# Hybrid decoder layer on one core: two weight passes of a feature chunk merged, a new chunk order, and units emitted by a clock per engine

## The chip, the cores and the metric

The kernel runs on one core of one Trainium2 chip. The core's engines each have an instruction queue of their own that is worked off in order: PE (matrix multiply), DVE (vector), ACT (activations), POOL (general purpose) and SP (which here only issues DMAs). The metric is the device time of one execution in microseconds (us), the median of several runs.

## The reference

One decoder layer over 256 tokens of width 1024, in float32. The tokens are RMS-normalised and multiplied by one wide input projection, whose columns feed three gated branches and three merge gates; each branch is projected back to 1024, the branches are summed under sigmoid gates, and an output projection, a residual add and a last RMSNorm follow.

```python
h = rms_norm(x, norm_g[layer])
(qa, ka, va, ga, ub, vb, gb, qc, gc, ma, mb, mc) = split_cols(h @ w_in[layer], IN_SPLITS)
qa = partial_rope(qa.reshape(B, S, MOBA_HEADS, HEAD_DIM), pos)
ka = partial_rope(ka.reshape(B, S, MOBA_HEADS, HEAD_DIM), pos)
va = va.reshape(B, S, MOBA_HEADS, HEAD_DIM)
out_a = moba_attention(qa, ka, va) * jax.nn.silu(ga)
out_b = gmlp_spatial_gate(ub, vb, gmlp_ln_g[layer], w_spatial[layer], b_spatial[layer]) * jax.nn.silu(gb)
mem_n = rms_norm(mem, mem_norm_g[layer])
out_c = memory_cross_attention(qc, mem_n, w_mem_kv[layer]) * jax.nn.silu(gc)
y = (jax.nn.sigmoid(ma) * (out_a @ w_branch_a[layer])
     + jax.nn.sigmoid(mb) * (out_b @ w_branch_b[layer])
     + jax.nn.sigmoid(mc) * (out_c @ w_branch_c[layer]))
x = x + y @ w_out[layer]
...
return rms_norm(x, final_norm_g)
```

Branch A has 6 heads of 128 with causal softmax attention (with 256 tokens there is a single block, so it is plain causal attention), branch B mixes 6 groups of 128 channels over chunks of 128 tokens, branch C has 4 heads of cross-attention into 256 memory tokens.

## The kernel before

**Products in three passes.** Every large product is made in a reduced float32 format (float32r). To keep precision, each operand is split into hi (rounded to that format) and lo (the rest), and a product is three passes accumulated in PSUM: hi·hi, hi·lo and lo·hi. The helper `mm3` (line 279) issues the three, so lines 280, 281 and 282 carry nearly all matmuls.

**Chunks.** The weights come from HBM as 52 pieces of two chunks each; a chunk is 128 × 1024 values and is the step of the main loop (line 784). There are 106 chunks. Per chunk, ACT writes hi (line 130), DVE writes lo (line 134), and PE multiplies. The splits run three chunks ahead of PE (`LEAD`), in four buffers of hi and of lo (`SPL`), so the hi of chunk c + 3 can start when PE has left chunk c − 1. The first four chunks are split before the loop.

There are four kinds of chunk. A *token* chunk (`mm_tok`, line 294) holds weights for 512 output columns and a quarter of the depth: the tokens are the stationary operand, the weights stream, 12 passes of 512 columns. A *feature* chunk (`mm_fea`, line 350) holds weights for 128 output features and the whole depth of 1024 in 8 steps of k: the weights are stationary and the 256 tokens stream, so 8 × 3 = 24 passes of 256 columns; the result lies with features on the partitions and is copied out of a PSUM bank by one ACT instruction. *Branch* and *output* chunks (`mm_br`, `mm_out`) stream weights like token chunks. Large products use four PSUM banks (`acc`) in turn, small ones four others (`aux`).

The order of the chunks (lines 251 to 272) is: 12 token chunks for the values of A and B (vvb); then per head q and k of A and two light ones out of ub and ga; then qc, mk (feature), mv (token), gc, gb (feature), 24 token chunks for the merge gates (sig), 16 branch chunks, 8 output chunks. Of these 42 are feature chunks.

The tokens for the first 12 chunks are not yet divided by their row norm (hh, hl); from chunk 12 on, normalised ones (nh, nl) are used. To make them, ACT squares and sums the rows (line 209), the reciprocal root becomes a diagonal, PE broadcasts it (line 226), ACT copies it out (line 228), POOL multiplies (line 421), ACT and DVE make hi and lo (lines 231 and 234).

**Units.** All small work (norms, rotation, attention, gates) is cut into named units. A planner written in Python (`Units`, line 46) decides, while the program is built, where each unit goes into the engines' queues. Before and after the matmuls of each chunk its `slot` goes through the list: a unit is emitted if the units it follows are done by at least `gap` chunks and if its cost, summed per engine, fits the room of one chunk. A unit holds work of several engines at once: the scores of a head, for instance, are matmuls, the maximum on DVE and the exponential on ACT. The rooms and the gaps are:

```python
U = Units(2, (1.3, 1.4, 1.35, 2.5), (0.3, 0.8, 0.6, 1.0))
```

Since each queue is in order, an emitted unit that is not ready holds up all that stands behind it on its engine.

**Activations.** SiLU of the gates ga, gc and gb and the sigmoid of sig are applied by ACT as it copies the product out of PSUM (lines 382, 385 and 322); the softmax uses Exp (line 484) and is normalised on DVE (line 495). ACT loads a table when it changes between such functions.

Of the kernel before, what the change touches and what calls it, by code (L numbers as in the profile page):

```python
# [32 lines left out]
D = 1024  # L33
S = 256
# [10 lines left out]

class Units:
# [5 lines left out]
    def __init__(self, gap, room, slack):  # L52
        self.gap, self.room, self.slack = gap, room, slack
        self.used = [0.0] * 4
        self.todo, self.done = [], {}

    def add(self, name, fn, after=(), cost=(0, 0, 0, 0), gap=None, before=(), first=False):
        unit = (name, fn, tuple(after), cost, self.gap if gap is None else gap, tuple(before))
        self.todo.insert(0 if first else len(self.todo), unit)

    def slot(self, i, pe):

        if not pe:
            self.used = [max(0.0, x - r) for x, r in zip(self.used, self.room)]
        rest = []
        todo, self.todo = self.todo, []
        for u in todo:
            name, fn, after, cost, gap, before = u
            if pe == (cost[0] > 0) and all(a in self.done and self.done[a] + gap <= i for a in after) \
# [5 lines left out]
                self.used = [x + c for x, c in zip(self.used, cost)]  # L75
            else:
                rest.append(u)
        self.todo += rest
# [3 lines left out]
def tile_hybrid_layer(ctx: ExitStack, tc: tile.TileContext, xw, memT, mem, x, fin_g, ln_g, w, w_sp, b_sp, rope, out):  # L82
# [112 lines left out]
    hh = act.tile([128, KD, S], F32R, name="hh", tag="hh")  # L195
    hl = act.tile([128, KD, S], F32R, name="hl", tag="hl")

    def sq_tile():
        return work.tile([128, S], F32, name="sq", tag="sq", bufs=2)
# [11 lines left out]
    def rms_rows(acc, dst):  # L211
        rt = work.tile([128, 2], F32, name="rt", tag="rt")
        nc.scalar.activation(rt, acc, AF.Sqrt, bias=eps, scale=1.0 / D)
        nc.vector.reciprocal(dst, rt)

    def rms_diag(r, name):
        dg = work.tile([128, 2, 128], F32, name="dg", tag="sq", bufs=2)
        for t in range(2):
            nc.vector.tensor_scalar(dg[:, t, :], ident, r[:, t:t + 1], None, op0=OP.mult)
        bc["d" + name] = dg  # L220

    def rms_bcast(name):

        p = bank()
        for t in range(2):
            nc.tensor.matmul(p[:, tsl(t)], ones, bc["d" + name][:, t, :], start=True, stop=True)  # L226
        bc[name] = work.tile([128, S], F32, name="bc", tag="ssq", bufs=2)
        nc.scalar.activation(bc[name], p[:, 0:S], AF.Copy)  # L228
# [23 lines left out]
    for g in range(3):  # L252
        chunks += [("tok", "vvb", g * 512, 2 * i) for i in range(4)]

    light = [("fea", "ub", g) for g in range(GB)] + [("fea", "ga", g) for g in range(HA)]
    for h in range(HA):
        chunks += [("fea", "q", h), ("fea", "k", h)] + light[2 * h:2 * h + 2]
    chunks += [("fea", "qc", h) for h in range(HC)]
    chunks += [("fea", "mk", h) for h in range(HC)]
    chunks += [("tok", "mv", 0, 2 * i) for i in range(4)]  # L260
    chunks += [("fea", "gc", g) for g in range(HC)]
    chunks += [("fea", "gb", g) for g in range(GB)]
# [521 lines left out]
    for c in range(n_br + 4):  # L784
# [3 lines left out]
        if s > 3:  # L788
            split(s)
# [116 lines left out]
```

## Time and profile before

| | |
|---|---|
| median of 3 runs | 331.46 us (331.08 to 537.75) |
| the profiled execution's own time | 330.89 us |
| its span, first to last instruction | 329.1 us |
| mean granted clock of PE | 0.997 |
| busy: PE, DVE, ACT, POOL | 321.7, 222.9, 191.2, 39.7 us |
| read from HBM | 61.55 MB, 190 GB/s over the span |

The profile is of one execution. Busy time is the union of an engine's instructions; matmuls are pipelined, so that a row's mean (285 ns for 256 columns) is longer than the distance to the next one. In a row of a group stand the line, engine, operation, what is written and read, the shape and the count; then busy us in total, mean ns of one, and the engine's idle time just before with what ended it. A row of a line's instructions has the durations in ns as min/median/max, then the first and the last start in us. In a timeline row stand the start and the duration in us.

### The profile page before, as it was taken

The page shows a single profiled execution, that of the slowest core. Times are in us where ns is not written, and L with a number is a line of the kernel's source. Part 1 is how long each engine was busy: PE and PEld are TensorE (multiplying, and loading weights), DVE is VectorE, ACT ScalarE, POOL GpSimd, SP SyncE. Part 2 cuts the span into 40 slices and gives each one's busy share as a digit, 9 for nine tenths or more (in the row PEclk, how much of TensorE's full clock was granted, in tenths as well). Part 3 has the DMA queues.
Part 4 walks back from the last instruction along what each step waited for, and adds up shares of the span by engine and source line. Part 5 has one row for each costly group of instructions (what it writes and reads, how often), then busy time and mean ns, then how long its engine had stood idle before and what let it go on. Part 6 is the DMA issues. An engine that isn't in the chain of part 4 may idle for free.

```text
span 329.1 us, 5062 instructions
## 1 busy us (share of the span) xinstructions
PE 321.7 (98%) x1999; PEld 289.3 (88%) x1999; DVE 222.9 (68%) x339; ACT 191.2 (58%) x315; POOL 39.7 (12%) x42
## 2 busy tenths in 40 slices
PE   8999999999999999999999999999999999999992
PEld 4888899999999999988999988888888888888882
DVE  4965869978867898678694755354435469768552
ACT  4779769465885666546964466535554633533433
POOL 0008210000001090100026430000000000000022
PEclk9999999999999999999999999999999999999998
DMA  7999875564433372533656264655465555463003
GB/s 286 392 423 333 341 295 178 207 209 170 134 127 130 127 257 71 201 136 132 245 177 224 66 223 138 247 159 223 147 238 177 205 187 197 135 247 129 0 1 128
DMA packets 10727, 62.91 MB, mean 191 GB/s; under 512 B 1200, under 2 KB 1584, under 8 KB 4176
## 3 DMA queue, kind: packets, MB, share of 16 engines
q1 hardware_dynamic: 10416, 62.08, 52.1%
q10 hardware_dynamic: 288, 0.52, 0.4%
q8 instruction: 15, 0.25, 0.3%
q14 instruction: 8, 0.07, 0.1%
HBM read 61.55 MB, written 1.05 MB: 190 GB/s over the span
## 4 chain that ended last, share of the span: by engine, by line
PE 97%; DVE 1%; ACT 0%; issue 0%; DVEq 0%
PE acc L280 26%; PE acc L282 26%; PE acc L281 26%; PE acc L309 4%; PE aux L280 3%; PE aux L282 3%; PE aux L281 3%; PE aux L472 2%; PE aux L193 1%; PE aux L641 1%; PE aux L512 0%; PE aux L545 0%; ACT jk L757 0%; PE aux L226 0%; DVE xk L755 0%; DVE xk L777 0%
## 5 line engine op out<-in xcount | busy, mean ns | idle before, releaser
L134 DVE TENSOR_TENSOR lo<-raw,hi 128x1024 fp32r<-128x1024 f32 x102 | 127.6, 1254 | 71.2 <-ACT hi L130 67.4
L130 ACT ACTIVATE hi<-raw 128x1024 fp32r<-128x1024 f32 x102 | 107.6, 1057 | 55.3 <-PE acc L282 47.4
L280 PE MATMUL acc<-nh,hi 128*128 128x256 f32 x304 | 86.6, 285 | 0.0
L282 PE MATMUL acc<-nh,lo 128*128 128x256 f32 x304 | 86.0, 283 | 0.0
L281 PE MATMUL acc<-nl,hi 128*128 128x256 f32 x304 | 85.9, 283 | 0.0
L281 PEld LDWEIGHTS acc<-nl,hi 128*128 128x128 f32 x304 | 58.2, 192 | 0.0
L280 PEld LDWEIGHTS acc<-nh,hi 128*128 128x128 f32 x304 | 58.2, 191 | 0.0
L282 PEld LDWEIGHTS acc<-nh,lo 128*128 128x128 f32 x304 | 58.2, 191 | 0.0
L280 PE MATMUL acc<-hi,nh 128*128 128x512 f32 x96 | 37.5, 390 | 0.0
L282 PE MATMUL acc<-hi,nl 128*128 128x512 f32 x96 | 37.4, 389 | 0.0
L281 PE MATMUL acc<-lo,nh 128*128 128x512 f32 x96 | 37.3, 389 | 0.0
L282 PEld LDWEIGHTS acc<-hi,nl 128*128 128x128 f32 x96 | 18.0, 188 | 3.8
L281 PEld LDWEIGHTS acc<-lo,nh 128*128 128x128 f32 x96 | 18.0, 188 | 3.7
L280 PEld LDWEIGHTS acc<-hi,nh 128*128 128x128 f32 x96 | 18.0, 188 | 3.7
L761 POOL TENSOR_TENSOR xk<-xk,fing 128x512 f32<-128x512 f32 (+1 forms) x4 | 4.0, 1010 | 126.4 <-ACT jk L757 126.4
L650 POOL TENSOR_TENSOR qk<-qk,ga 128x512 f32<-128x512 f32 x3 | 4.0, 1328 | 71.7 <-ACT qk L546 71.7
L421 POOL TENSOR_TENSOR st<-st,bc 128x256 f32<-128x256 f32 x8 | 7.9, 1027 | 24.4 <-ACT bc L228 24.4
L322 ACT ACTIVATE sig<-acc 128x512 f32<-128x512 f32 x12 | 7.1, 598 | 5.3 <-PE acc L282 4.9
L280 PE MATMUL acc<-hi,ah 128*128 128x512 f32 x24 | 9.4, 393 | 0.0
L282 PE MATMUL acc<-hi,al 128*128 128x512 f32 x24 | 9.4, 390 | 0.0
L281 PE MATMUL acc<-lo,ah 128*128 128x512 f32 x24 | 9.3, 389 | 0.0
L280 PE MATMUL acc<-hi,obh 128*128 128x512 f32 x24 | 9.3, 389 | 0.0
(207 smaller groups left out, 590.1 us busy)
## 6 DMA issues: line engine op xcount, KB each, us to landing
raw<-in_w_dram SPq DMA_DIRECT2D x50, 1024.0 KB, 4.8
st<-in_xw_dram SPq DMA_DIRECT2D x6, 384.0 KB, 6.2
raw<-in_w_dram SPq DMA_DIRECT2D x2, 512.0 KB, 7.9
xk<-in_x_dram SPq DMA_DIRECT2D x1, 1024.0 KB, 11.7
mt<-in_memT_dram SPq DMA_DIRECT2D x2, 512.0 KB, 7.6
mm<-in_mem_dram SPq DMA_DIRECT2D x2, 512.0 KB, 9.1
out_dram<-xk SPq DMA_DIRECT2D x2, 384.0 KB, 2.5
fing<-in_fin_g_dram SPq DMA_DIRECT2D x1, 512.0 KB, 5.6
```

The lines of the kernel that those rows point to most:

```text
L130: nc.scalar.activation(hi[c][:, a:b], raw[c // 2][:, o + a:o + b], AF.Copy)
L134: nc.vector.tensor_tensor(lo[c][:, a:b], raw[c // 2][:, o + a:o + b], hi[c][:, a:b].bitcast(F32), OP.subtract)
L193: nc.tensor.matmul(wp, warm[:, 0:128], warm, start=True, stop=True)
L280: nc.tensor.matmul(p, s_hi, m_hi, start=first, stop=False)
L281: nc.tensor.matmul(p, s_hi, m_lo, start=False, stop=False)
L282: nc.tensor.matmul(p, s_lo, m_hi, start=False, stop=last)
L309: nc.tensor.matmul(acc[name, o][t][:, a:b], src[:, k, tsl(t)], wt[c][:, i * 512 + a:i * 512 + b], start=k + n == 0, stop=k == KD - 1 and n ...
L322: nc.scalar.activation(V[f"sig{t}"][:, o, :], acc[name, o][t], AF.Sigmoid)
L421: U.add(f"nm{k}", lambda k=k: nc.gpsimd.tensor_tensor(x_k(k), x_k(k), bc["x"], OP.mult), after=["xrms"], gap=1)
L472: nc.tensor.transpose(p[:, hsl(j)], src, ident)
L650: nc.gpsimd.tensor_tensor(src, src, g, OP.mult)
L761: nc.gpsimd.tensor_tensor(z, z, V["fing"][:, a:b], OP.mult)
```

## The change

**Merged pass.** The hi and lo of the tokens now lie next to each other in one tile for each k (`pair`: n, and likewise h, m, a and y). In a feature chunk each step of k is two passes: the weights' hi against all 512 columns [hi | lo] into a whole PSUM bank, and the weights' lo against the 256 hi columns into the bank's first half. The two halves are added at the end (`join`): ACT copies the first half to SBUF, and a later unit on DVE adds the second half to it from PSUM.

**Chunk order.** The four-chunk groups of the merge gates are spread: the first group (sig 0) follows the first four q and k chunks, the second follows mv, the other four stay at the end. gc goes between the second and third group of heads, four of the ga behind the third, the rest of ga behind sig 1. The host lays the weights out in this order.

**Clock.** The planner keeps a time per engine. A unit is now work of one engine with a duration; what spanned several engines is a chain of such units. A unit that isn't for PE is emitted when its engine is at most 2.5 us ahead of PE's clock and its inputs are ready by 0.3 us after the engine would reach it; a PE unit when its inputs have been ready for 0.8 us. Some units have a chunk number by which they are emitted in any case.

**Activations.** Gates are copied out without an activation; SiLU runs later behind a barrier (`exps`) that follows the last exponential, the sigmoid of the first two gate groups behind the last SiLU. The softmax is normalised on ACT in place of DVE.

```diff
+def plan():
+    p = [("vvb", g) for g in range(3)]
+    for r in range(3):
+        p += [(n, h) for h in (2 * r, 2 * r + 1) for n in ("q", "k")]
+        p += ([("sig", 0)], [("gc", h) for h in range(HC)], [("ga", h) for h in range(4)])[r]
+        p += [("ub", 2 * r + i) for i in range(2)]
+    p += [(n, h) for n in ("qc", "mk") for h in range(HC)]
+    p += [("mv", 0), ("sig", 1)]
+    p += [("ga", h) for h in range(4, HA)]
+    p += [("gb", g) for g in range(GB)]
+    return p + [("sig", g) for g in range(2, 6)]
...
-    def __init__(self, gap, room, slack):
-        self.gap, self.room, self.slack = gap, room, slack
-        self.used = [0.0] * 4
-        self.todo, self.done = [], {}
-    def add(self, name, fn, after=(), cost=(0, 0, 0, 0), gap=None, before=(), first=False):
-        unit = (name, fn, tuple(after), cost, self.gap if gap is None else gap, tuple(before))
-        self.todo.insert(0 if first else len(self.todo), unit)
+    def __init__(self, start, ahead, margin):
+        self.t, self.ahead, self.margin = [start] * 4, ahead, margin
+        self.todo, self.end = [], {}
+    def add(self, name, e, us, fn, after=(), first=False, wait=0.0, due=10 ** 6):
+        self.todo.insert(0 if first else len(self.todo), (name, e, us, fn, tuple(after), wait, due))
+    def chain(self, name, *parts, after=(), due=10 ** 6):
+        for i, (e, us, fn) in enumerate(parts):
+            n = name if i == len(parts) - 1 else f"{name}.{i}"
+            self.add(n, e, us, fn, after, due=due)
+            after = [n]
+    def run(self, e, us, ready=0.0):
+        self.t[e] = max(self.t[e], ready) + us
+        return self.t[e]
+    def ready(self, after):
+        return max([self.end[a] for a in after], default=0.0) + 0.1
+    def fits(self, u, i, pe, now):
+        name, e, us, fn, after, wait, due = u
+        if pe != (e == PE) or any(a not in self.end for a in after):
+            return False
+        if i >= due or e is None:
+            return True
+        if pe:
+            return self.ready(after) + self.margin <= now
+        return self.t[e] <= now + self.ahead and self.ready(after) <= max(now, self.t[e]) + 0.3
-                    and all(a in self.done for a in before) \
-                    and all(c == 0 or x == 0 or x + c <= r + s
-                            for c, x, r, s in zip(cost, self.used, self.room, self.slack)):
+        now, u = self.t[PE], True
+        while u:
+            if pe:
+                now = self.t[PE]
+            u = next((u for u in self.todo if self.fits(u, i, pe, now)), None)
+            if u:
+                self.todo.remove(u)
+                name, e, us, fn, after, wait, due = u
+                at = self.ready(after)
+                self.end[name] = (at if e is None else self.run(e, us, at)) + wait
                 fn()
-                self.done[name] = i
...
+    def pair(name, tag, n):
+        t = slot_tile(name, [128, n, 2, S], tag, F32R)
+        V[name + "h"], V[name + "l"] = t[:, :, 0, :], t[:, :, 1, :]
+        return V[name + "h"], V[name + "l"]
...
-    U = Units(2, (1.3, 1.4, 1.35, 2.5), (0.3, 0.8, 0.6, 1.0))
+    U = Units(4.5, 2.5, 0.8)
...
-    def later(name, fn, *args, cost=(0, 0.5, 0, 0), after=()):
-        U.add(name, lambda: fn(*args), cost=cost, after=after, gap=1, first=True)
+    def later(name, e, us, fn, *args, after=()):
+        U.add(name, e, us, lambda: fn(*args), after=list(after) + [f"c{now[0]}"], first=True)
...
             for t in range(2):
-                if o == 0:
-                    slot_tile(f"sig{t}", [128, 6, 512], f"p{1 + t}")
-                nc.scalar.activation(V[f"sig{t}"][:, o, :], acc[name, o][t], AF.Sigmoid)
+                nc.scalar.activation(sig[g][:, t, :], acc[name, o][t], AF.Sigmoid if g > 1 else AF.Copy)
+                U.run(ACT, 0.62, U.end[f"c{c}"])
+            if g < 2:
+                U.add(f"sgm{g}", ACT, 1.1, lambda: nc.scalar.activation(sig[g], sig[g], AF.Sigmoid), after=["silu"])
...
     def mm_fea(c):
         _, name, h = chunks[c]
-        sh, sl = (V["mh"], V["ml"]) if name == "mk" else (V["nh"], V["nl"])
-        p = acc_bank()[:, 0:S]
+        src = V["m" if name == "mk" else "n"]
+        p = acc_bank()
+        pa, pb = p[:, 0:S], p[:, S:2 * S]
         for k in range(KD):
-            mm3(p, hi[c][:, hsl(k)], lo[c][:, hsl(k)], sh[:, k, :], sl[:, k, :], k == 0, k == KD - 1)
+            passes = [(p, hi[c][:, hsl(k)], src[:, k].rearrange("p a s -> p (a s)")),
+                      (pa, lo[c][:, hsl(k)], src[:, k, 0, :])]
+            if k == KD - 1:
+                passes.reverse()
+            for i, (o, wt, m) in enumerate(passes):
+                nc.tensor.matmul(o, wt, m, start=k + i == 0, stop=k + i == KD)
+        def join(dst):
+            nc.scalar.activation(dst, pa, AF.Copy)
+            U.end[f"e{c}"] = U.run(ACT, 0.4, U.end[f"c{c}"])
+            later(f"{name}{h}", DVE, 0.42, lambda: nc.vector.tensor_tensor(dst, dst, pb, OP.add), after=[f"e{c}"])
...
-            nc.scalar.activation(V["qk"][:, h, int(name == "k"), :], p, AF.Copy)
+            join(V["qk"][:, h, int(name == "k"), :])
...
+            tmp = join_tile()
+            join(tmp)
+            i = int(name == "mk")
+            dh, dl = V["cx"][:, i, h, :], V[("qcl", "mkl")[i]][:, h, :]
+            if i:
+                later(f"mkf{h}", DVE, 0.42, lambda: nc.vector.tensor_tensor(tmp, tmp, bc["m"], OP.mult),
+                      after=[f"mk{h}"])
+            later(f"{name}h{h}", ACT, 0.4, lambda: nc.scalar.activation(dh, tmp, AF.Copy),
+                  after=[f"mkf{h}" if i else f"qc{h}"])
+            later(f"{name}l{h}", DVE, 0.42, sub_lo, dl, tmp, dh, after=[f"{name}h{h}"])
...
+            g = join_tile()
+            join(g)
+            u = V["ub"][:, h, :]
+            U.chain(f"gbs{h}", (ACT, 0.4, lambda: nc.scalar.activation(g, g, AF.Silu)),
+                    (POOL, 0.75, lambda: nc.gpsimd.tensor_tensor(u, u, g, OP.mult)), after=[f"gb{h}", "exps"])
...
+        nc.scalar.activation(bc[name], bc["p" + name][:, 0:S], AF.Copy)
+    def rms_all(name, r):
...
-    U.add("nxa", lambda: (slot_tile("nh", [128, KD, S], "nh", F32R), slot_tile("nl", [128, KD, S], "nl", F32R)))
+    U.end["load_x"] = 21.0
+    U.add("nxa", None, 0, lambda: pair("n", "n2", KD))
     for t in range(2):
-        U.add(f"xsq{t}", lambda t=t: row_squares(V["xk"][:, t, :], ssx[:, t:t + 1], act.tile(
-            [128, D], F32, name="jx", tag=("och", "ocl")[t])), after=["c4"], gap=1, cost=(0, 0, 0.95, 0))
-    U.add("xrow", lambda: (rms_rows(ssx, rstd), rms_diag(rstd, "x")), after=["xsq0", "xsq1"], gap=0,
-          cost=(0, 0.6, 0.05, 0))
-    U.add("xrms", lambda: rms_bcast("x"), after=["xrow"], gap=1, cost=(0.5, 0, 0.4, 0))
+        U.add(f"xsq{t}", ACT, 1.25, lambda t=t: row_squares(V["xk"][:, t, :], ssx[:, t:t + 1], act.tile(
+            [128, D], F32, name="jx", tag=("och", "ocl")[t])), after=["load_x"])
+    U.chain("xrow", *rms_rows(ssx, rstd, rts[:, 0:2]), after=["xsq0", "xsq1"])
+    U.chain("xrms", *rms_all("x", rstd), after=["xrow"])
...
-        U.add(f"nm{k}", lambda k=k: nc.gpsimd.tensor_tensor(x_k(k), x_k(k), bc["x"], OP.mult),
-              after=["xrms"], gap=1)
+        U.add(f"nm{k}", POOL, 1.05, lambda k=k: nc.gpsimd.tensor_tensor(x_k(k), x_k(k), bc["x"], OP.mult),
+              after=["xrms"], due=7)
...
-        U.add(f"nxh{k}", lambda k=k: gain_hi(x_k(k), gain[:, k:k + 1], V["nh"][:, k, :]), cost=(0, 0, 0.4, 0),
-              after=[f"nm{k}", "nxa"], gap=1)
+        U.add(f"nxh{k}", ACT, 0.42, lambda k=k: gain_hi(x_k(k), gain[:, k:k + 1], V["nh"][:, k, :]),
+              after=[f"nm{k}", "nxa"], due=8 + k // 2)
...
-        nc.vector.reciprocal(rc, sm)
+        p, _, off = ST[kind, h]
         for t in range(2):
             pt = p[:, off[t]:off[t + 1]]
-            nc.vector.tensor_scalar(pt, pt, rc[:, t:t + 1], None, op0=OP.mult)
+            nc.scalar.activation(pt, pt, AF.Copy, scale=ST[kind + "r", h][:, t:t + 1])
     def a_split_hi(h):
...
+        U.chain(f"qsl{h}", (DVE, 1.45, lambda h=h: rope_a(h)), (DVE, 1.45, lambda h=h: rope_b(h)),
+                (ACT, 0.5, lambda h=h: a_split_hi(h)), (DVE, 0.55, lambda h=h: a_split_lo(h)),
+                after=[f"q{h}", f"k{h}", "consts"] + back("v", h) + ([f"as{h - 2}.0"] if h > 1 else []))
+        U.chain(f"as{h}", (PE, 0.55, lambda h=h: a_scores(h)), (DVE, 0.9, lambda h=h: a_max(h)),
+                (ACT, 1.0, lambda h=h: softmax_exp("a", h)), after=[f"qsl{h}", "sqrts"] + back("p", h))
+        U.chain(f"an{h}", (DVE, 0.2, lambda h=h: softmax_sum("a", h)), (ACT, 0.75, lambda h=h: softmax_norm("a", h)),
+                after=[f"as{h}"])
+        U.chain(f"ap{h}", (PE, 0.33, lambda h=h: a_pT(h)), (ACT, 0.72, lambda h=h: a_pT_out(h)),
+                after=[f"an{h}"] + back("v", h))
+        U.chain(f"av{h}", (DVE, 0.42, lambda h=h: p_lo("a", h, S)), (PE, 0.55, lambda h=h: a_pv(h)),
+                (ACT, 0.4, lambda h=h: a_out(h)), after=[f"ap{h}"])
+    def ln_centre(t):
...
+    U.add("exps", None, 0, lambda: None, after=[f"as{h}" for h in range(HA)] + [f"cs{h}" for h in range(HC)])
+    for name, n in (("gc", HC), ("ga", HA)):
+        U.add(name + "s", ACT, n * 0.25, lambda name=name: nc.scalar.activation(V[name], V[name], AF.Silu),
+              after=["exps"] + [f"{name}{i}" for i in range(n)])
+    U.add("silu", None, 0, lambda: None, after=["gcs", "gas"] + [f"gbs{g}" for g in range(GB)])
...
         U.slot(c, False)
         if s > 3:
             split(s)
+            U.end[f"s{s}"] = U.run(DVE, 1.23, U.run(ACT, 1.05, max(U.end.get(f"c{s - SPL}", 0), 9.0 + 1.45 * s)))
         if s % 2 == 1 and 3 < s // 2 + 2 < n_pieces:
+        U.end[f"c{c}"] = U.run(PE, 2.78 if kind == "fea" else 2.73, U.end.get(f"s{c}", 0.0))
         if kind == "tok":
```

More of the change, by code (lines that the diff above doesn't have):

```diff
@@ L328, in mm_tok @@
                 nc.scalar.activation(h, p, AF.Copy, scale=f)
-                later(f"mvl{t}", scaled_lo, l, p, f, h)
-            U.done[f"{name}.{o}"] = now[0]
+                U.run(ACT, 0.62, U.end[f"c{c}"])
+                later(f"mvl{t}", DVE, 0.7, scaled_lo, l, p, f, h)
+            U.end[f"{name}.{o}"] = U.end[f"c{c}"]
     def evict_v(o):
@@ L562, in ln_rstd @@
             nc.vector.bn_aggr(lst[:, t, :], st)
-        rt = work.tile([128, 2], F32, name="rt", tag="rt")
-        nc.scalar.activation(rt, lst[:, :, 1], AF.Sqrt, bias=eps, scale=1.0)
-        nc.vector.reciprocal(lrs, rt)
-    def ln_apply(t):
+    U.chain("lnr", (DVE, 2.4, ln_stats),
+            (ACT, 0.3, lambda: nc.scalar.activation(lrt, lst[:, :, 1], AF.Sqrt, bias=eps, scale=1.0)),
+            (DVE, 0.2, lambda: nc.vector.reciprocal(lrs, lrt)), after=["vvb.1024"])
+    U.add("sqrts", None, 0, lambda: None, after=["lnr", "mrow"])
@@ new lines, in tile_hybrid_layer, with mem_units @@
+    U.chain("mrms", *rms_all("m", rstm), after=["mrow"])
+    mk0 = chunks.index(("fea", "mk", 0))
+    def mem_units():
+        U.add("mxa", None, 0, mem_alloc, after=["vvb.1024"])
+        for k in range(KD):
+            g = gains[:, KD + k:KD + k + 1]
+            U.add(f"mxh{k}", ACT, 0.42, lambda k=k, g=g: gain_hi(mem_k(k), g, V["mh"][:, k, :]),
+                  after=["load_mem", "mxa"], due=mk0 - 5 + k // 2)
+            U.add(f"mxl{k}", DVE, 0.5, lambda k=k, g=g: gain_lo(mem_k(k), g, V["mh"][:, k, :], V["ml"][:, k, :]),
+                  after=[f"mxh{k}"], due=mk0 - 5 + k // 2)
@@ L635, in mix_unit @@
     def mix_unit(i):
-        p = bank()
+        ST["mp", i] = p = bank()
         pv = p.rearrange("p (g t s) -> p g t s", g=2, t=2)
@@ L659, in lo_part @@
             nc.vector.tensor_tensor(dl, src, dh.bitcast(F32), OP.subtract)
-        U.add(name + "h", hi_part, after=after, gap=1, cost=(0, 0, 0.5, 0))
-        U.add(name, lo_part, after=[name + "h"], gap=1, cost=(0, 0.6, 0, 0))
+        U.chain(name, (ACT, 0.6, hi_part), (DVE, 0.68, lo_part), after=after)
     def alloc(*specs):
@@ L685, in tile_hybrid_layer @@
     for i in range(3):
-        U.add(f"mix{i}", lambda i=i: mix_unit(i), after=["lna0", "lna1"], cost=(0.87, 0.7, 0, 0),
-              before=[f"cp{HC - 1}", f"gb{2 * i + 1}"], gap=2)
+        U.chain(f"mix{i}", (PE, 0.82, lambda i=i: mix_unit(i)), (DVE, 0.85, lambda i=i: mix_bias(i)),
+                after=["lna0", "lna1", f"cp{HC - 1}"])
     for i in range(3):
-        U.add(f"mg{i}", lambda i=i: nc.gpsimd.tensor_tensor(
+        U.add(f"mg{i}", POOL, 1.3, lambda i=i: nc.gpsimd.tensor_tensor(
```

313 lines of the change are left out of this document (148 added, 165 removed).

## The prediction

> **What bounds the kernel now.** I read the page first (busy shares, then the chain of waits), then the busy time by stage, and last the single matmuls of two stages.
>
> ```profile
> span 329.1 us, 5062 instructions
> ...
> PE 321.7 (98%) x1999; PEld 289.3 (88%) x1999; DVE 222.9 (68%) x339; ACT 191.2 (58%) x315; POOL 39.7 (12%) x42
> ...
> PE 97%; DVE 1%; ACT 0%; issue 0%; DVEq 0%
> ```
>
> The matrix engine is busy for 98% of the span and carries 97% of the chain that ends last. Nothing off PE can shorten the time; only shorter PE work can, and work elsewhere matters only if it makes PE wait. A busy PE is not yet a PE at its peak, so the next look is at the distance between the starts of neighbouring matmuls, in a feature chunk (256 columns) and in a token chunk (512 columns).
>
> ```profile
> 106.89 0.28 PE L280 MATMUL acc<-nh,hi 128*128 128x256 f32 x1
> ...
> 107.25 0.28 PE L280 MATMUL acc<-nh,hi 128*128 128x256 f32 x1
> ...
> 107.49 0.28 PE L282 MATMUL acc<-nh,lo 128*128 128x256 f32 x1
> ...
> 227.76 0.39 PE L281 MATMUL acc<-lo,nh 128*128 128x512 f32 x1
> ...
> 233.88 0.39 PE L281 MATMUL acc<-lo,nh 128*128 128x512 f32 x1
> ...
> 311.67 0.28 PE L282 MATMUL aux<-hi,yl 128*128 128x256 f32 x1
> 311.79 0.40 PE L280 MATMUL aux<-hi,yh 128*128 128x512 f32 x1
> ```
>
> From 106.89 to 107.49 lie five steps: 0.120 us per 256-column pass. From 227.76 to 233.88 lie 27: 0.227 us per 512-column pass. Two passes of 256 thus cost 0.240, one of 512 0.227: each pass carries about 13 ns besides its columns. The last two rows show the neighbourhood that the change makes the rule: a 256-column pass followed by a 512-column one, again 0.12 apart.
>
> Whether the other engines have room is told by the busy time of the feature stretch (38.70 to 160.70) and of a stretch of token chunks behind it. Columns: stretch and its length, then busy us and count of PE, PEld, DVE, ACT, POOL, then granted clock, DMA share, GB/s.
>
> ```profile
> 38.70:160.70 122.00, 122.00 (x979) 119.82 (x979) 98.45 (x184) 81.43 (x162) 12.22 (x11) 1.00 0.49 174
> ...
> 212.00:256.00 44.00, 44.00 (x196) 36.44 (x195) 19.61 (x16) 21.71 (x26) 0.00 (x0) 1.00 0.55 197
> ```
>
> DVE is at 81% in the first and at 45% in the second; the granted clock is 1.00 in both. The feature stretch is the place where something could begin to starve PE.
>
> **The merged pass.** A feature chunk has eight steps over k. Before, a step is three 256-column passes: 3 × 0.120 = 0.360. After, it is one of 512 (the weights' hi against hi and lo of the tokens, side by side in the new paired tile) and one of 256 (the weights' lo against hi): 0.227 + 0.120 = 0.347. The columns streamed are the same; what goes is one pass and one weight load of three. That is 8 × 0.013 = 0.104 us a chunk.
>
> ```profile
> L280 PE MATMUL acc<-nh,hi 128*128 128x256 f32 x304 | 86.6, 285 | 0.0
> ...
> L280 PE MATMUL acc<-mh,hi 128*128 128x256 f32 x32 | 9.3, 290 | 0.0
> ```
>
> 304 + 32 = 336 passes at eight a chunk are 42 feature chunks, so the saving is 42 × 0.104 = 4.4 us, all of it on PE. The bounds: if the 256-column pass among long ones costs only half of a long one (0.1135), a step is 0.3405 and the saving 42 × 8 × 0.0195 = 6.6 us; if the pass that follows a different length takes its 13 ns back, it is 0. I take 0.347, since the 311.67 row shows that very pair at 0.12. Token, branch and output chunks keep their passes.
>
> The Trainium skill, "TensorE: Matmul & The Clock Gate", section "Back-to-back issue gap", speaks against the merge being worth this much: a warm gap is the columns over 2.4 GHz plus about 2.5 ns, so a removed pass would give back 2.5 ns, and the sum 42 × 8 × 2.5 ns = 0.8 us in place of 4.4. This trace disagrees with both of its gaps (it gives 109 and 216 ns, the rows have 120 and 227).
>
> **The halves summed at eviction.** The product now sits in two halves of a PSUM bank. ACT copies one half out, as it copied the result before; DVE then adds the other half.
>
> ```profile
> L359 ACT ACTIVATE qk<-acc 128x256 f32<-128x256 f32 x12 | 4.6, 380 | 8.1 <-PE acc L282 6.5 <-issue 1.6
> ...
> L288 DVE TENSOR_TENSOR ptl<-aux,pth 128x256 fp32r<-128x256 f32 x6 | 2.4, 409 | 0.0
> ...
> L495 DVE TENSOR_SCALAR p<-p,rc 128x256 f32<-128x256 f32 x14 | 5.6, 425 | 0.1
> ...
> L495 DVE TENSOR_SCALAR p<-p,rc 128x128 f32<-128x128 f32 x6 | 2.0, 341 | 0.2
> ...
> L134 DVE TENSOR_TENSOR lo<-raw,hi 128x1024 fp32r<-128x1024 f32 x102 | 127.6, 1254 | 71.2 <-ACT hi L130 67.4 <-PE acc L281 2.9
> ...
> L130 ACT ACTIVATE hi<-raw 128x1024 fp32r<-128x1024 f32 x102 | 107.6, 1057 | 55.3 <-PE acc L282 47.4 <-PE aux L282 5.6 <-DMA raw<-in_w_dram 2.1
> ```
>
> No such add is in the trace; its nearest row is the 256-column subtraction that also reads PSUM, 409 ns. 42 of them are 17.2 us on DVE. The softmax normalising moves from DVE to ACT and takes 5.6 + 2.0 = 7.6 us off. In the chunks of the stretch quoted (34 feature chunks before; chunks 12 to 49 in the new order also hold 34) DVE goes from 98.45 to 98.45 + 34 × 0.41 − 7.6 = 104.8 us, while PE's stretch shrinks to 122 − 34 × 0.104 = 118.5: 88% in place of 81%. It fits, and what hides it is that DVE still has the lo half of a chunk ready before PE wants it. In the tightest place I found the lead is short:
>
> ```profile
> 104.92 1.21 DVE L134 TENSOR_TENSOR lo<-raw,hi 128x1024 fp32r<-128x1024 f32 x1
> ```
>
> That split belongs to chunk 34, whose first matmul is the 107.25 row: 1.1 us of lead, against some 4 to 6 elsewhere. What queues behind the add on DVE is the next lo split; what waits for the add is the PSUM bank, which the fourth chunk later takes over, 3 × 2.78 = 8.3 us on. The new planner puts such adds first in its list and lets DVE run at most 2.5 us ahead of PE's clock before it emits, so I cost this at nothing; if the cover goes, the price is that of the DVE rival below.
>
> ACT gains the normalising (20 activations at about 0.4, an estimate from the 380 ns row: 8 us), separate SiLU and sigmoid steps (about 7 us), and loses table loads, because the gates are copied out and activated later, behind one barrier after the last exponential:
>
> ```profile
> L484 ACT ACT_TABLE_LOAD x3 | 3.8, 1283 | 0.0
> L382 ACT ACT_TABLE_LOAD x3 | 3.8, 1283 | 0.1
> ```
>
> Four of these six go, 5.1 us. ACT ends near 191 + 15 − 5 = 201 of 326 us, 62%: nothing on the path either way.
>
> **The new chunk order and the clock.** Neither removes work from PE; they move when units reach the in-order queues. Two places can cost. First the start, where the normalised tokens must be ready for chunk 12, the first feature chunk.
>
> ```profile
> L209 ACT ACTIVATE jx<-xk x2: 1045/1054/1064, 18.9 to 20.0; 128x1024 f32<-128x1024 f32 x2
> ...
> 24.69 0.61 PE L226 MATMUL aux<-dg,ones 128*128 128x128 f32 x4
> ...
> L421 POOL TENSOR_TENSOR st<-st,bc x8: 744/758/1787, 25.8 to 32.7; 128x256 f32<-128x256 f32 x8
> ...
> L234 DVE SCALAR_TENSOR_TENSOR nl<-st,st,nh x4: 471/471/472, 35.9 to 38.2; 128x256 fp32r<-128x256 f32 x4
> ...
> 38.76 0.28 PE L280 MATMUL acc<-nh,hi 128*128 128x256 f32 x1
> ```
>
> Before, the broadcast of the row norms runs on PE at 24.69, behind chunk 6, and the last nl tile is done at 38.2 + 0.5 = 38.7, just as chunk 12 begins. By the constants in the diff, the clock starts chunk 4 at 14.8 + 1.05 + 1.23 = 17.08 and ends chunk 7 at 17.08 + 4 × 2.73 = 28.0; the squares wait for its 21.0 and so go out in slot 6, the reciprocal and diagonal in slot 7 with an end near 27.8, and with 0.1 and the margin of 0.8 that is 28.7: too late for chunk 7's slot, so the broadcast goes behind chunk 8. Two chunks of 2.72 later, POOL's eight products end near 33.4 + 5.4 = 38.8. ACT and DVE then still have the last hi and lo (0.4 and 0.47) to make, with the splits of chunks 12 to 14 emitted among them (1.06 and 1.25 each), so the last lo comes near 41; PE wants it at k = 7, 38.76 + 7 × 0.347 = 41.2. (PE does not wait for a whole tile: the hl tiles end at 13.8 by their row, and chunk 0 starts at 4.43.)
>
> ```profile
> L234 DVE SCALAR_TENSOR_TENSOR hl<-st,st,hh x4: 478/480/483, 10.3 to 13.3; 128x256 fp32r<-128x256 f32 x4
> ...
> 4.43 2.40 PE acc L309 x8
> ```
>
> It is a draw: 0 to 1 us, I take 0.5. On POOL the constants (mask and trigonometry) fall behind these products, and on SP the memory loads pass ahead of the trigonometry load; the first rotation waits for that, but PE has the four chunks of the first gate (16 to 19) in the meantime.
>
> Second, PE's small units (scores, transposes, values). Each is emitted once its input is 0.8 us old by the clock, so a clock that is wrong by more makes PE wait. They also break the stream of passes:
>
> ```profile
> 101.43 0.36 PE L280 MATMUL acc<-nh,hi 128*128 128x256 f32 x1
> 101.63 0.29 PE L281 MATMUL acc<-nl,hi 128*128 128x256 f32 x1
> ```
>
> Behind a transpose the second pass starts 0.20 after the first, 0.08 late. Units that ran in pairs may now run singly; some six more such breaks are 0.5 us. A gain is excluded up to the 2 us that the present breaks cost. I take 0.5 for breaks and waits, and keep 0 to 4 for the range.
>
> **The sum.** Against the profiled execution's own 330.89 us (span 329.1 and 1.8 around it): 330.89 − 4.4 + 0.5 + 0.5 = 327.5. The median of the runs, 331.46, is 0.6 higher and their lowest, 331.08, is 0.2 higher; I add 0.2 and predict 327.7.
>
> **The rivals.**
> - *Waits between the engines eat most of the gain.* For it: DVE at 88%, a lead that is down to 1.1 us in one place already, a clock whose prices are a few per cent under the rows (1.23 for the lo split, the row has 1.254). Against: PE waits for nothing in the feature stretch now, and such a lag heals whenever DVE idles. 2 to 4 us more: 329.5 to 331.5.
> - *DVE becomes the bound of the feature stretch*, and the kernel gets slower. DVE idles 23.6 us there now. If none of that can be used, since the in-order queue sits behind lo splits that wait for ACT (67.4 us in the kernel by the row), the stretch takes 98.45 + 23.55 + 13.9 − 7.6 = 128.3 in place of 118.5: 327.7 + 9.8 = 337.5. It decides once the lead of the lo split is used up in chunk after chunk. Against: the planner holds back whatever is not due, and behind the stretch DVE is at 45%.
> - *The merged pass saves nothing*, because the 13 ns come back where pass lengths alternate: 327.7 + 4.4 = 332.1. Against: the two pitches and the 311.67 row. By the Trainium skill's gap rule named above this would be 0.8 less, 331.3.
> - *The short pass hides wholly behind the long one* (a step of 0.3405): 327.7 − 2.2 = 325.5. For it: half of 0.227 is 0.1135. Against: the same row.
>
> **Chances and range.** The forecast (326.5 to 329) 0.61, the waits 0.20, the DVE bound 0.07, nothing saved 0.05, the hidden short pass 0.05, and 0.02 for anything else. The range from 325.4 to 331.3 leaves out the DVE bound, the upper end of the waits and part of the rest. Two per cent, about what a measurement of this kernel tells from no change, are 6.6 us: faster means under 324.8, which takes the 0.3405 step and fewer breaks (0.04); slower means over 338.1, the worse part of the DVE case and the unknown (0.06); the rest, 0.90, is within.
>
> **What would show it.** In the changed kernel's profile the feature chunks' neighbouring 512 and 256 passes should start 0.227 and 0.120 apart; PE's count should fall by 336 to about 1660; DVE's busy time should rise by about 10 us to 232 and ACT's table loads fall. The first feature chunk should start near 38.8 and may show a gap of up to 1 us at its last k. The prediction is wrong if PE shows gaps before feature chunks (DVE's lo released late), if a bank's add keeps a chunk waiting, or if the pass pitch differs from these two numbers.

## The result, and the profile after

The changed kernel takes 335.59 us (median of 4 runs, 334.33 to 337.25) against 331.27 for the kernel before. One run of the kernel before took 537.75 us, and the ratio leaves it out: 1.0142, with a 95% interval of 1.0116 to 1.0169. So the changed kernel is slower, by more than the noise and by less than 2%. The forecast was 327.7 with a range up to 331.3. The four runs lie in two pairs: 334.33 and 334.51 at a mean granted clock of 0.996, and 336.66 and 337.25 at 0.992 and 0.987. The profiled one is the 336.66, and its profile holds a stretch at half clock (below). That the 337.25 run holds one too, and the faster pair none, is inferred from their times and mean clocks.

The page of the changed kernel, its busy times and its chain of waits:

```profile
span 334.9 us, 4443 instructions
...
PE 321.3 (96%) x1663; PEld 271.7 (81%) x1663; DVE 231.1 (69%) x361; ACT 201.8 (60%) x349; POOL 40.7 (12%) x42
...
PE 83%; DMA 7%; ACT 3%; DVE 3%; issue 1%; POOL 1%; SPq 0%; DVEq 0%; ACTq 0%; POOLq 0%
```

PE has its 336 passes less (1663 in place of 1999), and DVE and ACT have gained what was worked out (231.1 and 201.8 us). But the chain no longer runs on PE alone: its share fell from 97% to 83%. What PE waited for is in its list of waits (us in total, times, longest):

```profile
PE acc L323 <- DVE qk L420: 3.0, 2, 1.8
PE aux L323 <- DVE y L331: 1.5, 1, 1.5
...
PE acc L414 <- DVE n L285: 0.9, 1, 0.9
```

Three places, all behind DVE. (Left out here are two rows in which PE waits at the very start: the warming matmuls, 1.3 us as before, and a first load that landed later, 0.5.) The first is in front of and inside chunk 16, the first chunk of the first merge gate, which writes two banks. In the timeline of PE the gap before each of its banks is plain, and the timeline of DVE shows what ends it:

```profile
51.14 0.39 PE L414 MATMUL acc<-n,hi 128*128 128x512 f32 x1
52.77 0.50 PE L323 MATMUL acc<-hi,n 128*128 128x512 f32 x1 [1.24 <-DVE qk L420]
...
53.34 0.40 PE L325 MATMUL acc<-hi,n 128*128 128x512 f32 x1
55.53 0.50 PE L323 MATMUL acc<-hi,n 128*128 128x512 f32 x1 [1.79 <-DVE qk L420]
```

```profile
45.64 1.22 DVE L180 TENSOR_TENSOR lo<-raw,hi 128x1024 fp32r<-128x1024 f32 x1 [0.91 <-ACT hi L176]
48.34 1.23 DVE L180 TENSOR_TENSOR lo<-raw,hi 128x1024 fp32r<-128x1024 f32 x1 [1.47 <-ACT hi L176]
51.16 1.23 DVE L180 TENSOR_TENSOR lo<-raw,hi 128x1024 fp32r<-128x1024 f32 x1 [1.60 <-ACT hi L176]
52.30 0.41 DVE L420 TENSOR_TENSOR qk<-qk,acc 128x256 f32<-128x256 f32 x1
53.91 1.23 DVE L180 TENSOR_TENSOR lo<-raw,hi 128x1024 fp32r<-128x1024 f32 x1 [1.20 <-ACT hi L176]
55.06 0.41 DVE L420 TENSOR_TENSOR qk<-qk,acc 128x256 f32<-128x256 f32 x1
```

Chunks 12 to 15 (q and k of heads 0 and 1) hold the four `acc` banks, and a bank is free only when its second half has been added. Chunk 12 ended at 42.9, but the first add of any of them runs at 52.30, 9.4 us later, behind the lo split of chunk 18, and PE goes on 0.06 us after its end. By the code it isn't even the add of chunk 12: `later` puts each new unit at the front of the planner's list, so that the newest add goes out first, and chunk 16 gets the bank that comes free first. DVE was not busy meanwhile: it idled 0.91, 1.47 and 1.60 us before those splits. The adds were not late because DVE had no time but because they stood too far back in DVE's queue. Against a distance of 0.227 from pass to pass the two gaps are 1.40 and 1.96 us.

Then comes the half clock: the granted clock is the third number from the right in these stretches of the changed kernel.

```profile
51.00:55.60 4.60, 1.57 (x8) 0.78 (x6) 3.12 (x4) 4.03 (x10) 2.27 (x6) 1.00 0.82 319
55.60:60.00 4.40, 4.40 (x13) 3.45 (x14) 0.00 (x0) 0.80 (x1) 0.00 (x0) 0.61 0.62 240
```

Behind the gaps the granted clock is 0.61 in the mean of 4.40 us, that is 3.4 us at half, and passes of 512 columns start 0.43 apart in place of 0.227. This costs another 1.7. The other two waits are 1.1 us inside chunk 12, at the last k but one (it waits for the nl tiles), and 1.6 us at 312 us, where an output chunk takes over a bank that a late subtraction still reads:

```profile
42.12 0.50 PE L414 MATMUL acc<-n,hi 128*128 128x512 f32 x1 [0.95 <-DVE n L285]
...
313.64 0.39 PE L323 MATMUL aux<-hi,y 128*128 128x256 f32 x1 [1.46 <-DVE y L331]
```

Adding up the difference of the two profiled spans, 334.9 − 329.1 = 5.8: gaps at the gate chunk 3.4, half clock 1.7, tail 1.6, chunk 12 with its two further breaks 1.3, the first load 0.5; less 2.5 for the merged pass (below). That is 6.0.

### The profile page after: what moved, and what is told of

It is laid out like the page before. It is cut to its first block, busy times and chain, and to the rows that moved or that the text cites. A ratio compares the mean times of both kernels' runs of the same rounds, so it can differ in the third digit from the quotient of the medians.

```text
span 334.9 us, 4443 instructions
## 1 busy us (share of the span) xinstructions
PE 321.3 (96%) x1663; PEld 271.7 (81%) x1663; DVE 231.1 (69%) x361; ACT 201.8 (60%) x349; POOL 40.7 (12%) x42
## 4 chain that ended last, share of the span: by engine, by line
PE 83%; DMA 7%; ACT 3%; DVE 3%; issue 1%; POOL 1%; SPq 0%; DVEq 0%; ACTq 0%; POOLq 0%
PE acc L414 35%; PE acc L323 12%; PE acc L324 12%; PE acc L325 12%; DMA raw<-in_w_dram 5%; PE aux L323 3%; PE aux L324 3%; PE aux L325 3%; DMA st<-in_xw_dram 2%; PE aux L539 2%; ACT hi L176 1%; DVE lo L180 1%; PE aux L748 1%; POOL st L490 1%; DVE n L285 1%
## 5 line engine op out<-in xcount | busy, mean ns | idle before, releaser
L414 PE MATMUL acc<-n,hi 128*128 128x512 f32 x304 | 107.6, 399 | 0.9 <-DVE n L285 0.9
L414 PE MATMUL acc<-n,lo 128*128 128x256 f32 x304 | 79.0, 280 | 0.0
L414 PEld LDWEIGHTS acc<-n,hi 128*128 128x128 f32 x304 | 55.7, 188 | 11.7 <-DVE n L285 1.5
L414 PEld LDWEIGHTS acc<-n,lo 128*128 128x128 f32 x304 | 57.4, 189 | 2.9
L323 PE MATMUL acc<-hi,n 128*128 128x512 f32 x80 | 32.3, 403 | 3.0 <-DVE qk L420 3.0
L324 PE MATMUL acc<-lo,n 128*128 128x512 f32 x80 | 31.9, 398 | 0.0
L325 PE MATMUL acc<-hi,n 128*128 128x512 f32 x80 | 31.8, 397 | 0.0
L323 PEld LDWEIGHTS acc<-hi,n 128*128 128x128 f32 x80 | 15.3, 191 | 6.9 <-DVE qk L420 3.8
L324 PEld LDWEIGHTS acc<-lo,n 128*128 128x128 f32 x80 | 15.5, 193 | 3.4 <-DVE lo L180 0.3
L325 PEld LDWEIGHTS acc<-hi,n 128*128 128x128 f32 x80 | 15.4, 193 | 3.3
L414 PE MATMUL acc<-m,hi 128*128 128x512 f32 x32 | 11.4, 400 | 0.0
L323 PE MATMUL acc<-hi,a 128*128 128x512 f32 x24 | 9.4, 393 | 0.0
L325 PE MATMUL acc<-hi,a 128*128 128x512 f32 x24 | 9.3, 389 | 0.0
```

The source lines that it names most:

```text
L323: nc.tensor.matmul(p, s_hi, m_hi, start=first, stop=False)
L324: nc.tensor.matmul(p, s_hi, m_lo, start=False, stop=False)
L325: nc.tensor.matmul(p, s_lo, m_hi, start=False, stop=last)
L414: nc.tensor.matmul(o, wt, m, start=k + i == 0, stop=k + i == KD)
```

## The experiments

**Theory A:** the merged pass is a gain, and the loss comes from three places where the clock lets a DVE step go out too late. **Rival B:** DVE has no room for the adds, and a wait cured in one place comes back in another.

### The half-adds right behind their chunk

```diff
-            later(f"{name}{h}", DVE, 0.42, lambda: nc.vector.tensor_tensor(dst, dst, pb, OP.add), after=[f"e{c}"])
+            U.add(f"{name}{h}", DVE, 0.42, lambda: nc.vector.tensor_tensor(dst, dst, pb, OP.add),
+                  after=[f"e{c}", f"c{c}"], first=True, due=c + 1)
```

> Only the emission of the 42 half-adds is changed: each is emitted in the slot right after its chunk, whatever DVE's clock says. Theory A (the planner held the adds of q0 and k0 back, because its DVE clock counts the waits behind ACT as work and so stands more than 2.5 us ahead; the first gate chunk then waits for their banks): the two gaps of 1.4 and 2.0 us at 51 to 55 us go, and with them the stretch of 3.4 us at half clock: about 331.0 us, against 334.4 (clock 0.996) to 337 (clock 0.987 to 0.992) for the changed kernel, and every run at a clock of 0.996 or more. Rival B (DVE has no room in the feature stretch, so that the adds take the place of lo splits): the gaps come back before feature chunks, 333.5 us or more.

Measured: 331.04 us, ratio to the kernel before 1.0012 (1.0001 to 1.0023). PE's list of waits has lost the qk row and keeps the other two:

```profile
PE aux L323 <- DVE y L331: 1.5, 1, 1.5
...
PE acc L414 <- DVE n L285: 0.9, 1, 0.9
```

DVE's timeline now has the four adds one by one behind the splits, from 44.10 on:

```profile
44.10 0.41 DVE L420 TENSOR_TENSOR qk<-qk,acc 128x256 f32<-128x256 f32 x1
...
51.82 0.41 DVE L420 TENSOR_TENSOR qk<-qk,acc 128x256 f32<-128x256 f32 x1
```

Nothing came back elsewhere: 3.4 us gone and no stretch at half clock, as A had it. B falls for this stretch.

### The limit of the clock

```diff
-    U = Units(4.5, 2.5, 0.8)
+    U = Units(4.5, 4.0, 0.8)
```

> One constant of the changed kernel: an engine may stand 4.0 us ahead of PE's clock in place of 2.5 when a unit is emitted. Theory A (DVE's clock stands just above the limit at chunks 13 to 15, since it counts the waits behind ACT's hi; with 4.0 the adds pass): the gaps at 51 to 55 us go, and those at chunk 12 (1.1 us) and in the tail (1.6 us) stay: about 331 us. Rival B (the limit is not what held them): the gaps at 51 to 55 us stay, 334 us or more.

Measured: 331.65 us (1.0023, 1.0008 to 1.0038). The first add runs at 44.68, each chunk's add goes out behind it, the gaps at the gate chunk are gone, those of chunk 12 (0.85) and of the tail (1.62) stay. So the condition "not more than 2.5 us ahead of PE" did hold the adds back. Worked through with the constants of the code, the planner has DVE 2.80, 2.63 and 2.55 us ahead of PE at chunks 13, 14 and 15, just over the limit, and 2.47 at chunk 16, where one add fits and takes DVE over the limit again. DVE's clock books each lo split behind ACT's hi and keeps that wait as time taken; ACT itself may be filled to the limit and one unit over, so DVE's clock stands above the limit while the engine idles.

### The subtraction of y right behind its transposes

```diff
-        U.chain(f"yt{half}{i}", (PE, 0.44, turn),
-                (ACT, 0.62, lambda: nc.scalar.activation(V["yh"][:, k, :], view(), AF.Copy)),
-                (DVE, 0.7, lambda: sub_lo(V["yl"][:, k, :], view(), V["yh"][:, k, :])), after=after)
+        U.add(f"yp{half}{i}", PE, 0.44, turn, after)
+        U.chain(f"yt{half}{i}", (ACT, 0.62, lambda: nc.scalar.activation(V["yh"][:, k, :], view(), AF.Copy)),
+                (DVE, 0.7, lambda: sub_lo(V["yl"][:, k, :], view(), V["yh"][:, k, :])), after=[f"yp{half}{i}"], due=0)
```

> Only the copy and the subtraction of the turned y are changed: both are emitted in the slot after their transposes, ahead of that slot's split. Theory A (the output chunk at 312 us waits 1.6 us for a PSUM bank that the late subtraction still reads): 1.6 us less than the changed kernel, 332.8 at the clock of 0.996. Rival B (PE waits for the turned values themselves or for DVE's load there): the gap stays within 0.4 us of 1.6, or appears one chunk later, 334 or more.

Measured: 334.42 us, 332.38 to 335.44, which alone says little, since the gaps at the gate chunk and their half clock are still there (the one run at a mean clock of 0.999 took 332.38, 2.0 less than the faster pair of the changed kernel). The trace decides. In the changed kernel the subtraction stood behind the lo split at 311.76; in this one it stands ahead of it (two rows of each kernel's DVE timeline, the changed kernel first):

```profile
311.76 1.22 DVE L180 TENSOR_TENSOR lo<-raw,hi 128x1024 fp32r<-128x1024 f32 x1 [2.91 <-ACT hi L176]
312.91 1.28 DVE L331 TENSOR_TENSOR y<-aux,y 128x512 fp32r<-128x512 f32 x2
```

```profile
310.15 1.29 DVE L331 TENSOR_TENSOR y<-aux,y 128x512 fp32r<-128x512 f32 x2 [1.47 <-ACT y L825]
311.59 1.22 DVE L180 TENSOR_TENSOR lo<-raw,hi 128x1024 fp32r<-128x1024 f32 x1 [0.15 <-ACT hi L176]
```

PE's wait for y is gone from its list, and no other took its place: 1.6 us.

### The row squares earlier

```diff
-    U.end["load_x"] = 21.0
+    U.end["load_x"] = 18.5
```

> Only one constant of the clock is changed: the row squares may go out at 18.5 of its time in place of 21.0. Theory A (the broadcast of the row norms went out two chunks later than before and made the last nl tile late for chunk 12): the gap of 1.1 us at 41 us and its two breaks go, 1.2 us less than the changed kernel, 333.2 at the clock of 0.996. Rival B (the wait at chunk 12 comes from DVE's splits of chunks 13 and 14 ahead of the last tile, whenever the broadcast runs): the gap stays at 1 us, 334.4.

Measured: 330.29 us (0.9984, 0.9974 to 0.9994), 3 us better than expected. The copy of the broadcast norms runs at 28.2 in place of 31.4, and the gap at chunk 12 is gone, as A had it. But so are the two gaps at the gate chunk: the first half-add runs at 42.06.

```profile
42.06 0.42 DVE L420 TENSOR_TENSOR qk<-qk,acc 128x256 f32<-128x256 f32 x1
```

The expectation treated the two faults as separate, and they are not. With the norms a chunk earlier, the units that are forced out by their due numbers load the clocks of ACT and DVE earlier, and by chunk 13 DVE's clock is back under the limit. Worked through with the code's constants, DVE's clock then stands 2.13 us ahead at chunk 13 in place of 2.80. That link is argued from the code and from the limit's own run; what is shown is that either edit removes the gaps.

### All three edits

The three edits above together (adds, y, row squares).

> The three edits together. Theory A (three separate emission faults, the merged pass itself a gain): 334.4 - 3.4 - 1.6 - 1.2 = 328.2 us, below the kernel before by about 1%. Rival B (DVE is the bound of the feature stretch and the stalls move): 331.5 us or more.

Measured: 327.76 us, ratio 0.9905 (0.989 to 0.992): faster than the kernel before by 1%, and the gain is there. PE's list of waits has one row left, of the warming matmuls at the start:

```profile
PE aux L239 <- DVE warm L229: 1.3, 1, 1.3
```

DVE in the feature stretch (38.40 to 157.00; columns as before) is at 99.81 of 118.6 us, 84%, and makes PE wait nowhere.

```profile
38.40:157.00 118.60, 118.60 (x690) 103.93 (x689) 99.81 (x189) 78.95 (x160) 6.21 (x8) 1.00 0.52 188
```

### The merge undone

Two kernels have three passes of 256 columns and no add, one with the faults of the changed kernel and one with the edits of y and of the row squares.

```diff
-            passes = [(p, hi[c][:, hsl(k)], src[:, k].rearrange("p a s -> p (a s)")),
-                      (pa, lo[c][:, hsl(k)], src[:, k, 0, :])]
...
+            mm3(pa, hi[c][:, hsl(k)], lo[c][:, hsl(k)], src[:, k, 0, :], src[:, k, 1, :], k == 0, k == KD - 1)
```

> The merge alone is undone in the changed kernel: three passes of 256 columns into one half bank and no add on DVE; chunk order, clock and tiles stay. Theory A (the merged pass saves 0.06 us a chunk, but its adds hold the banks that the first gate chunk waits for): the two gaps at 51 to 55 us go (3.4 us, and the half clock), the feature chunks take 2.88 again (+2.6 us): 333 to 334 us. Rival B (the gaps come from the chunk order and the clock, not from the adds): the gaps stay, 337 or more.

> The edits of the row squares and of the y units, and the merge undone (three passes of 256 columns, no half-adds): what chunk order and clock are worth without the merge. Theory A (the merge is worth 42 x 0.06 = 2.5 us of the three-edit kernel's gain and order and clock next to nothing): 327.8 + 2.5 = 330.3 us, level with the kernel before at 330.8. Rival B (the gain over the kernel before comes from order and clock): 328.5 or less.

Measured: 333.68 us (1.0086, 1.0065 to 1.0106) for the first: no gap at the gate chunk, the other two stay, and an undisturbed feature chunk is back at 2.88 us from 2.82. The second: 330.73 us (0.9993, 0.9982 to 1.0005), level with the kernel before. So without the merge the chunk order, the clock and the moved activations together are worth nothing here once their faults are out, and the merge is worth the difference to its counterpart with the same waits: 333.68 − 331.04 = 2.6 us (the kernel with the adds moved), 330.73 − 327.76 = 3.0 us (the one with all three edits). The two kernels of each pair were timed on different occasions; by their ratios to the kernel before, timed alongside each, it is 2.4 and 2.9.

### The passes grouped

```diff
-            if k == KD - 1:
-                passes.reverse()
...
+        passes = wide[:-1] + short + wide[-1:]
```

> Only the order of a feature chunk's 16 passes is changed: seven of 512 columns, then the eight of 256, then the last of 512. The changed kernel's alternating passes start 233 (512, then 256) and 117 ns (256, then 512) apart, 350 a step, where the prediction had 227 + 120 = 347. Theory A (each change of length costs some ns): 8 x 227 + 8 x 120 = 2.776 us a chunk in place of 2.82, some 1 to 1.8 us less over 42 chunks. Rival B (the extra goes with the wide pass or with reading the paired tile): the chunk stays at 2.82 and the time at that of the changed kernel.

> The three edits (half-adds emitted right behind their chunk, copy and subtraction of y right behind its transposes, row squares from 18.5) and the grouped passes of a feature chunk. Theory A (each change of pass length costs about 3 ns; grouped, a chunk took 2.79 in place of 2.82): 327.8 - 42 x 0.03 = 326.5 us. Rival B (the grouping only brings the last nl tile's deadline forward, as it did alone at chunk 12): 327.8 or more, with a gap at 40 us.

Measured: alone 336.99 us, with the gaps of the changed kernel, a longer one at chunk 12 (all wide passes come first and want the last nl tile sooner) and 6.8 us at half clock in the profiled run; so the time tells nothing of the passes. Together with the three edits it is 327.08 us, ratio 0.9882 (0.9859 to 0.9905): the best kernel of this study, though its interval overlaps that of the three edits alone. The passes themselves can be read from the timelines. In the changed kernel they alternate:

```profile
43.26 0.40 PE L414 MATMUL acc<-n,hi 128*128 128x512 f32 x1
43.49 0.28 PE L414 MATMUL acc<-n,lo 128*128 128x256 f32 x1
43.61 0.40 PE L414 MATMUL acc<-n,hi 128*128 128x512 f32 x1
...
45.03 0.40 PE L414 MATMUL acc<-n,hi 128*128 128x512 f32 x1
```

Five steps from 43.26 to 45.03: 0.354 a step. In the grouped kernel with the three edits runs of eight follow each other:

```profile
69.03 2.00 PE L412 MATMUL acc<-n,hi 128*128 128x512 f32 x8
70.87 1.11 PE L412 MATMUL acc<-n,lo 128*128 128x256 f32 x8
71.82 2.00 PE L412 MATMUL acc<-n,hi 128*128 128x512 f32 x8
```

From 69.03 to 71.82 is one chunk, 2.79 us, 0.349 a step. Over all such pairs in the feature chunks of the changed kernel the median distance is 233 ns from a 512-column pass to a 256-column one and 117 back. In the grouped kernels it is 231 from one 512-column pass to the next and 120 between 256-column ones. So the alternation costs 0.03 us a chunk, as A had it; 42 chunks make 1.3 us, of which 0.7 to 0.8 were measured (by the times and by the ratios). A smaller rest goes with the wide pass itself, as B had it: also in a row the long pass stays above the 227 of a token chunk, and a grouped chunk takes 2.79, not 2.776. Why is open.

### The chunk order undone

```diff
+    light = [("ub", g) for g in range(GB)] + [("ga", h) for h in range(HA)]
+    for h in range(HA):
+        p += [("q", h), ("k", h)] + light[2 * h:2 * h + 2]
```

> The chunk order alone is undone: light chunks, gates and memory in the order of the kernel before; merged pass and clock stay. Theory A (the adds of the first chunks are emitted late whatever follows): chunk 16 is then a feature chunk that needs q0's bank only, so the first gap stays near 1.4 us and the next one shrinks; 332.5 to 334. Rival C (the first gate group is to blame, because it takes two banks at once): no gap at chunk 16, 331 or less. If late units pile up elsewhere, more.

Measured: 338.62 us (1.0234, 1.0217 to 1.0251), worse than the changed kernel and worse than either theory had it. Rival C falls: the first gate group is not to blame. With feature chunks only, each one from chunk 16 on needs one bank, the planner lets out one add a chunk from there to chunk 19, and five chunks in a row (16 to 20) wait 1.1 to 1.5 us for one. From PE's list of waits:

```profile
PE acc L413 <- DVE ub L419: 3.2, 3, 1.3
PE acc L413 <- DVE qk L419: 1.9, 2, 0.9
```

DVE's timeline shows the newest add going first:

```profile
51.77 0.41 DVE L419 TENSOR_TENSOR ub<-ub,acc 128x256 f32<-128x256 f32 x1
...
55.78 0.42 DVE L419 TENSOR_TENSOR qk<-qk,acc 128x256 f32<-128x256 f32 x1 [1.27 <-ACT qk L417]
```

The first add of all is one of ub, while q0 and k0 still hold their banks, and the second waits for the copy out of the chunk that has just ended. So each chunk waits for the one before it, not for the fourth before it. The late adds are the same; the new order even spared three of these gaps, because a gate group runs four chunks on two banks. I had counted one bank, not the row of them. A sixth wait is new here, 1.4 us at 216 us for a unit of DVE; the six gaps are 7.3 us against 3.4 in the changed kernel, which is 3.9 of the 4.2 us that this run took over 334.4.

### The merged pass alone in the kernel before

The core of the edit to the kernel before, beside the paired tiles:

```diff
+    def run_adds():
+        for unit, dst, half in adds:
+            nc.vector.tensor_tensor(dst, dst, half, OP.add)
+            U.done[unit] = now[0] - 1
+            U.used[1] += 0.42
+        adds.clear()
...
-    U = Units(2, (1.3, 1.4, 1.35, 2.5), (0.3, 0.8, 0.6, 1.0))
+    U = Units(2, (1.3, 1.7, 1.35, 2.5), (0.3, 0.9, 0.6, 1.0))
```

> The merged pass alone in the kernel before: paired tiles, merged pass, the half-adds emitted right behind their chunk, gates activated in place behind the add; chunk order and the old planner stay (its DVE room is 1.7 with a slack of 0.9, a rotation is counted as 1.7, so that all units still find a place). Theory A (the merged pass is a gain of 0.06 us a chunk where no add holds a bank): 331.3 - 2.6 = 328.7. Rival B (DVE at 88% of the stretch makes PE wait): 331 or more, with gaps before feature chunks.

Measured: 339.03 us (1.0245, 1.023 to 1.026). The feature chunk is 2.82 here too, but PE waits for DVE in other places:

```profile
PE aux L285 <- DVE ql L292: 3.0, 2, 1.9
PE aux L498 <- DVE p L521: 2.5, 4, 0.8
PE acc L285 <- DVE lo L139: 1.5, 1, 1.5
```

In the first two rows small PE units stand in the queue before their DVE input is ready; in the third a chunk of a merge gate, behind the feature stretch, waits for its lo split. With the rooms that I gave it, the old planner packs DVE (102.5 us busy of 122 in the feature stretch) and still emits PE's units a fixed number of chunks later. This looks like rival B, but the rooms are mine and no other setting was tried, so the run shows only that the merge without a matching planner can lose more than it brings. Whether the old planner could carry it stays open.

## Why the prediction was wrong

**The step that failed is "I cost this at nothing"**, on the half-adds. The parts it was built from held: the add takes 0.41 us, ACT's and DVE's busy times came out as worked (201 and 232 predicted, 201.8 and 231.1 measured), and DVE has room (84% in the kernel with the three edits). What was wrong is the reading of the clock's rule. I took "lets DVE run at most 2.5 us ahead" as a promise that an add goes out within 2.5 us. It is a condition for leaving it out: while DVE's clock stands above the limit, nothing that is not due goes out, and the lo splits, which do not ask the clock, keep lifting it. I had even named what waits for the add, the bank, with its 8.3 us; the first add came 9.4 us after the first chunk that needs one. "Puts such adds first in its list" also hid that the newest stands in front, so that the oldest banks stay taken. This step cost 3.4 us, and 5.1 in the profiled run, where the half clock followed.

**The merged pass was mis-sized.** The sum had 0.104 us a chunk and 4.4 in all; it measured 0.06 a chunk and 2.4 to 3.0. The 311.67 row showed one pair at a change of length, to two decimals, and only from short to long; from long to short, which no row showed, it is 233 ns where passes alternate. The direction held. The Trainium skill's gap rule ("TensorE: Matmul & The Clock Gate", section "Back-to-back issue gap"), by which it would have been 0.8, does not fit the undone merge either; the section gives that rule for an isolated matmul.

**The chain to chunk 12 was right in mechanism and just past the upper end of its size.** The broadcast did go out behind chunk 8 (the copy of it at 31.4 in place of 25.3), and the nl tiles were late: 1.1 us and 0.2 of breaks, where I took 0.5 out of 0 to 1. POOL's eight products ended at 40.2, not 38.8, and the lo split of a later chunk stood ahead of the last two tiles on DVE. That the same lateness would lift the clocks and so hold back the adds was not seen.

**The tail was missed.** I priced y's units nowhere, that is at nothing. Cutting a unit into a chain put its DVE part behind the next lo split, and a bank was held 1.6 us too long.

**The rivals.** The waits between the engines came, but at 6.6 us (334.4 less 327.8), not 2 to 4. The DVE bound did not: DVE idled before the gate chunk's gaps and before the tail's; only at the gap in chunk 12 was it busy, with a lo split, and that gap went when the norms came earlier. (The lead of 1.1 us that I showed is the shortest of its stretch; the others lie between 1.8 and 7.7, wider than my "4 to 6".) What the forecast described, a merged pass with nothing in its way, is the kernel with the three edits: 327.76 us; that the sums agree is partly chance, as the smaller gain there meets none of the 1.0 us of waits.

## What to carry to other kernels

Before an instruction is called hidden, find the buffer it releases and the place in the queue where it is emitted; an engine's idle time does not help a step that stands behind later work. A planner that keeps one time per engine and counts waits in it will think an idle engine full, so steps that release a shared buffer should have a due number. And a new order of small steps should be read for the last chunks as carefully as for the first.

## What was not expected of the hardware

Two idle stretches of PE of 1.24 and 1.79 us with only three passes between them were followed by 3.4 us at half clock in the profiled run of the changed kernel (336.66 us, against 334.33 and 334.51 in the runs at a mean clock of 0.996), and the profiled run of the changed kernel with grouped passes had 6.8 us of it. Five waits of 0.9 to 1.3 us, some 4 us apart, in the run with the old chunk order were followed by none: its granted clock stayed at 1.00 from 49 to 72 us. The Trainium skill, "TensorE: Matmul & The Clock Gate", section "HAM oscillation — how this bites in real kernels", asks for idle gaps above about 3.4 us for that; here neither gap was so long, only both together came near. Gaps of 3.4 us thus cost 5.1. Passes of 512 and 256 columns that alternate start 233 and 117 ns apart, 350 a pair; the same passes of a feature chunk in rows of equal length 231 and 120, and those of a token chunk of the kernel before 227.
